# A hybrid mixer layer on one core: whole-row opening loads, dots ahead of the copies, and a planner with one shared transfer pipe

## The chip, the core and the metric

The kernel runs on one core of a Trainium2 chip. A core has a matrix engine (TensorE, PE in the profile), a vector engine (VectorE, DVE), a scalar engine (ScalarE, ACT), a general engine (GpSimd, POOL) and a queue engine (SyncE, SP) that issues most transfers. Operands lie in SBUF, matmul results in PSUM, inputs and outputs in HBM. The metric is the device time of the one program in microseconds, as the median of several runs. A separate profiled execution supplies the trace.

## The reference

The kernel computes one decoder layer and a final norm for a sequence of 1024 tokens and 1024 channels, in float32. Cut to what matters:

```
mod = silu(c) @ mod_w + mod_b                     # 1024 x 3072
shift, scale, gate = split(mod, 3)
h = rmsnorm(x, norm_g) * (1 + scale) + shift
u = h @ w_in                                      # 1024 x 5120
cv, cg, cs, lx, ls = split(u, 5)
v = causal_depthwise_conv(cv * sigmoid(cg), 31 taps)
v = silu(layernorm(v))
y_conv = (v @ pw2_w + pw2_b) * silu(cs)
xs = causal_depthwise_conv(lx, 4 taps)
r, i = sigmoid(block_diagonal(xs))                # two gates, 8 heads
hs = linear_scan(a = exp(-8 r softplus(-lam)), sqrt(1 - a*a) * i * xs)
y_lru = hs * silu(ls)
x = x + (1 + gate) * (concat(y_conv, y_lru) @ w_out)
return rmsnorm(x, final_g)
```

## The kernel before

Channels lie on the 128 partitions and tokens along the free dimension, so the 1024 x 1024 activations are eight tiles of 128 x 1024. Every float32 product is made from rounded parts: an operand is split into a high part (a cast on ACT, `hi`) and a remainder (a subtraction on DVE or POOL, `lo`), and a product takes three matmuls, high by high, high by remainder and remainder by high. A weight tile therefore costs a load, a cast (`whi`) and a subtraction (`wlo`), and six matmuls of 512 columns for each of eight channel tiles.

The work has these stages.

1. **Opening.** For each channel tile k three loads come in: 128 rows of the scale matrix (`s`k, tile `modw`), the input (`x`k) and the weights of the first four output tiles (`w`k or, two at a time, `W`k, tile `fraw`). `LOADS` gives their order. c, after silu, is spread over all partitions by 16 small matmuls into PSUM (`spread_c`, tile `c_row`), and ACT copies it to SBUF (`sc`). A dot of `modw` with the spread gives the scale of the channel tile (`dot`; `first_dot` for tile 0 reads PSUM directly, in two halves). From it follows `gs`, then `uh` and `ul`, the high part and remainder of x times `gs`. With them PE makes the products `first` (line 747). Small matmuls of ones (`idle_mm`, `IDLE` of them) keep PE busy before that. The first tile of x comes in two halves of 512 tokens and w0, w1 in separate loads.
2. **Row norm.** Squares of x are summed, PE sums them over channels and spreads the reciprocal root over partitions (`token_stats`, `rbc`). The shift matrix (`h`0 to `h`7) is dotted in the same way, and three further weight tiles (`NEXT`) are run on the scaled input before the shifted input `hh`, `hl` exists.
3. **Slots.** The list `slots` runs over the remaining tiles of w_in, the gates of the eight recurrence heads (`gates`) and the eight lru tiles of w_out. PE works through them one after another (line 472). The evacuations, the depthwise convolutions (`conv_tile`), the gates and the scans run beside it on ACT and DVE. In three of eight convolutions (`POOLED`) ACT makes the tap products and POOL-issued transfers add them up in SBUF; the last three operations fold them together (`FOLD`). Eight dots for the output gate run in the slots from `GM` on (`gate_mod`, engine `GDOT`). Weight remainders of the slots before number `EARLY` are made on POOL.
4. **Normalisation and pw2, then w_out.** The eight convolution tiles are added to `csum` in the order `SUMS`, then come mean, variance and silu, and the two remaining projections as pair products with fewer multiplications (`pair_products`, line 594; `papw` and `pbpw` are its PSUM tiles for pw2).
5. **End.** The last norm is made for the token ranges in `END`. For the last range `rstd` sums the squares with matmuls and spreads the reciprocal root (`spread`, line 685, tile `finbc`). ACT copies `finbc` to SBUF (`bc`) for the two tiles of channels that POOL finishes, and DVE reads `finbc` for the other six.

The order on every engine is not written by hand. Each operation is registered with an engine, an estimated cost, a priority and its reads and writes, and `Plan.order` simulates the five engines and puts the ready operation of lowest priority number next. `until` holds the time at which an engine is free, `done` the time at which a result is there, `releases` the buffers that come free. There are 47 large SBUF buffers, three PSUM tiles of two banks (`mm`) and two of one (`acc`). In the simulation of before an SP load occupies SP for its bytes, and the accumulating transfers of POOL have a pipe of their own (`adder`). Names such as `RES`, `HRES` and `SPARE` are buffers that stay in reserve when an operation asks for one.

Of the kernel before, what the change touches and what calls it, by code (L numbers as in the profile page):

```python
# [33 lines left out]
NEXT = (("in", LS), ("in", CS), ("in", CS + 1))  # L34
EW = FW + len(NEXT) * P
# [20 lines left out]
SUMS = (0, 1, 3, 2, 6, 4, 7, 5)  # L56
QRES = 4
AHEAD = 4
IDLE, IDLE0 = 15, 4
WARM = (5, 2)  # L60
LANDING, MARGIN = 5.0, 2.0
SP0 = 3.6
SPP = 30
PAD = 16
GLO = "DVE"
GDOT = "DVE"
FOLD = "DVE"
EARLY = 10
ISSUE, FLIGHT, RATE = 1.0, 10.0, 3.5
GM = 22  # L70
TAPP = -15
# [5 lines left out]
LOADS = "s0 x0 w0 s1 x1 w1 W2 s2 x2 s3 x3 W4 s4 x4 s5 x5 W6 s6 x6 s7 x7 h0 h1 h2 h3 h4 h5 h6 h7".split()  # L77
# [20 lines left out]
class Plan:  # L98
# [5 lines left out]
    TICK, BUSY = 3.4133, 3060  # L104

    def __init__(self, pools):
        self.pools = pools
        self.ops, self.writer, self.readers, self.adder = [], {}, {}, 0.0
# [46 lines left out]
    def order(self):  # L155
# [3 lines left out]
        until = {"PE": 1.0, "ACT": 2.0, "DVE": 2.9, "POOL": 1.1, "SP": SP0}  # L159
# [4 lines left out]
        releases, out, table, t, ticks = [], [], None, 0.0, {}  # L164
# [34 lines left out]
        while left:  # L199
# [3 lines left out]
            for e in engines:  # L203
# [69 lines left out]
def hymba_layer(ctx: ExitStack, tc: tile.TileContext, xT, vecs, mod_w, w_first, w_in,  # L273
# [137 lines left out]
    extra = {0: [2, 3], 1: [4], 2: [5], 3: [6], 4: [7]}  # L411
    late_cs = {5, 6, 7}
    for i in range(KT):
        slots.append(("in", LX + i))
        if i > 0:
            slots.append(("in", LS + i))
        if ("in", CS + i) not in NEXT and i not in late_cs:
            slots.append(("in", CS + i))
        if i == KT - 1:
            slots.append(("in", CS + 5))  # L420
        slots.append(("gate", i))
        for j in extra.get(i, []):
            slots += [("in", CG + j), ("in", CV + j)]
    slots += [("in", CS + 6), ("in", CS + 7)]
# [239 lines left out]
    def rstd(prio, sqs, a, e, ps, o, after=(), warm=()):  # L664
# [6 lines left out]

        idle = mm_tile("idle") if warm else None
# [10 lines left out]
        def spread():  # L683
# [11 lines left out]
        return wk, S.op("PE", 0.22 * nb, spread, prio, [rs], wk, columns=4 * P * nb)  # L695
# [64 lines left out]
    for i, ld in enumerate(LOADS):  # L760
# [6 lines left out]
        elif ld[0] in "wW":  # L767
# [6 lines left out]
            for j in range(k, k + nk):  # L774
                due[f"w{j}"] = p
                jj = j % 2
                ACT(p, fw_part(hi, j), fw_part(rw, j), "copy", FW, r=[(rw, jj)], w=[(hi, jj)])
                SUB(p, "DVE", fw_part(lo, j), fw_part(rw, j), fw_part(hi, j), FW,
                    r=[(rw, jj), (hi, jj)], w=[(lo, jj)])
        else:  # L780
            for a, e in START if k == 0 else ((0, T),):
                DMA(p + 1.5 * (k == 0 < a), part(xt[k], a, e), lambda k=k, a=a, e=e: xT[k * P:(k + 1) * P, a:e],
# [15 lines left out]
    def first_dot(p):  # L798
# [12 lines left out]
    for z in (0, 1):  # L811
        ACT(-101, half(sc, z), half(ps_c[z], 0), "copy", H, r=[ps_c[z]], w=[(sc, z)])
    begun, uhs, uls, scaled, split_u, last_u = {}, [], [], [], [], {}
    for k in range(KT):
        p = due[f"s{k}"]
        a_ = col(macc, KT + k)
        if k == 0:
            first_dot(p)
        else:
            dot(SCALE[k], p, KT + k, split_u[:1] if k == 1 else [])  # L820
        S.op("DVE", 0.2, lambda k=k, a_=a_: dve.scalar_tensor_tensor(
# [59 lines left out]
    for k, sq in enumerate(sqs):  # L881
        S.op("PE", 0.23 * KT, lambda sq=sq, k=k: stats(sq, k), RSP, [sq], wk,
# [4 lines left out]
    for a, e in START:  # L887
        spread = S.op("PE", 0.22 * ((e - a) // P), lambda a=a, e=e: spread_mm(a, e), RSP,
                      [("st", 0)], wk, columns=4 * (e - a))
        ACT(RSP, part(rbc, a, e), part(psb, 0, e - a), "copy", e - a, r=wk,  # L890
            w=halves(rbc, a, e))
# [571 lines left out]
```

## Time and profile before

| | |
|---|---|
| median of 3 runs | 741.27 us (740.9 to 742.06) |
| the profiled execution | 741.66 us |
| its span, first to last instruction | 739.8 us |
| granted TensorE clock over the span | 0.997 |
| busy in the span | PE 728.5, DVE 637.9, ACT 441.4, POOL 115.1 us |
| HBM read, written | 64.16 MB, 12.58 MB |

A row of the timeline holds the start and the duration in microseconds, the engine, the line of the kernel, the operation, what it writes and reads, and in brackets the idle time before it and what ended that. A row of the groups holds a count, the busy time and the mean in nanoseconds, then the idle time before the group. Matmuls overlap in the pipeline: one of 512 columns is shown as 0.39 us while the next starts 0.23 us later. "PEld" is the loading of weights into PE, "SPq" the queue of SP. Tile names in the profile stand without their numbers.

### The profile page before, as it was taken

The page shows a single profiled execution, that of the slowest core. Times are in us where ns is not written, and L with a number is a line of the kernel's source. Part 1 is how long each engine was busy: PE and PEld are TensorE (multiplying, and loading weights), DVE is VectorE, ACT ScalarE, POOL GpSimd, SP SyncE. Part 2 cuts the span into 40 slices and gives each one's busy share as a digit, 9 for nine tenths or more (in the row PEclk, how much of TensorE's full clock was granted, in tenths as well). Part 3 has the DMA queues.
Part 4 walks back from the last instruction along what each step waited for, and adds up shares of the span by engine and source line. Part 5 has one row for each costly group of instructions (what it writes and reads, how often), then busy time and mean ns, then how long its engine had stood idle before and what let it go on. Part 6 is the DMA issues. An engine that isn't in the chain of part 4 may idle for free.

```text
span 739.8 us, 8931 instructions
## 1 busy us (share of the span) xinstructions
PE 728.5 (98%) x3314; PEld 605.0 (82%) x3314; DVE 637.9 (86%) x847; ACT 441.4 (60%) x546; POOL 115.1 (16%) x116
## 2 busy tenths in 40 slices
PE   8999999999999999999999999999999999999996
PEld 7788888887888888888887888878888888877886
DVE  6999999988899788888499997978799867999945
ACT  6570597658867857946939777734754224455422
POOL 0023020220331330432215111010000000000003
PEclk9999999999999999999999999999999999999998
DMA  9953025664798899698872556425233430623206
GB/s 324 400 190 114 0 87 121 148 137 99 137 223 201 197 220 260 163 236 161 177 163 54 127 112 185 153 103 199 86 114 114 172 113 1 227 80 120 86 1 228
DMA packets 37340, 111.59 MB, mean 151 GB/s; under 512 B 4144, under 2 KB 12848, under 8 KB 37296
## 3 DMA queue, kind: packets, MB, share of 16 engines
q1 hardware_dynamic: 23904, 75.97, 29.0%
q0 software_dynamic: 12528, 34.26, 25.8%
q10 hardware_dynamic: 864, 0.79, 0.3%
q8 instruction: 26, 0.43, 0.2%
q14 instruction: 18, 0.15, 0.1%
HBM read 64.16 MB, written 12.58 MB: 104 GB/s over the span
## 4 chain that ended last, share of the span: by engine, by line
PE 88%; DVE 7%; ACT 1%; DMA 1%; issue 1%; SPq 0%; DVEq 0%
PE ps L472 65%; PE papw L594 5%; PE pbpw L594 4%; PE first L747 4%; PE pbout L594 2%; PE paout L594 2%; PE gate L1149 2%; PE out L655 2%; DMA fraw<-in_w_first_dram 1%; DVE fin L336 1%; PE late L747 1%; DVE rawout L344 1%; DVE l34out L344 1%; DVE yu L344 1%; DVE yt L344 0%
## 5 line engine op out<-in xcount | busy, mean ns | idle before, releaser
L472 PE MATMUL ps<-uh,whi 128*128 128x512 f32 x576 | 177.7, 390 | 0.6 <-ACT sls L325 0.6
L472 PE MATMUL ps<-ul,whi 128*128 128x512 f32 x576 | 177.5, 389 | 0.0
L472 PE MATMUL ps<-uh,wlo 128*128 128x512 f32 x576 | 177.5, 389 | 0.0
L472 PEld LDWEIGHTS ps<-uh,whi 128*128 128x128 f32 x576 | 107.9, 188 | 23.6 <-ACT sls L325 1.5
L472 PEld LDWEIGHTS ps<-uh,wlo 128*128 128x128 f32 x576 | 108.1, 188 | 22.5
L472 PEld LDWEIGHTS ps<-ul,whi 128*128 128x128 f32 x576 | 108.1, 188 | 22.4
L317 ACT CAST whi<-raw 128x1024 fp32r<-128x1024 f32 x46 | 48.1, 1051 | 66.1 <-PE ps L472 48.4
L349 POOL DMA_DIRECT2D es<-cq x45 | 40.5, 914 | 164.7 <-ACT cq L325 126.9
L325 ACT ACT_TABLE_LOAD x47 | 60.3, 1283 | 2.1 <-PEq L1455 0.7
L349 POOL DMA_DIRECT2D oo<-co x42 | 39.5, 946 | 122.9 <-ACT co L325 52.2
L344 DVE TENSOR_TENSOR wlo<-raw,whi 128x1024 fp32r<-128x1024 f32 x40 | 48.7, 1219 | 10.8 <-ACT whi L317 10.6
L336 DVE SCALAR_TENSOR_TENSOR cacc<-v,V,cacc 128x511 f32<-128x511 f32 (+14 forms) x75 | 55.8, 744 | 0.4
L336 DVE SCALAR_TENSOR_TENSOR caccs<-c,wsum,caccs 128x511 f32<-128x511 f32 (+6 forms) x70 | 52.1, 745 | 3.4 <-ACT caccs L325 2.4
L336 DVE SCALAR_TENSOR_TENSOR caccs<-v,V,caccs 128x511 f32<-128x511 f32 (+6 forms) x70 | 52.2, 746 | 0.9
L344 POOL TENSOR_TENSOR o<-fin,bc 128x256 f32<-128x256 f32 (+1 forms) x8 | 7.3, 938 | 244.6 <-ACT bc L317 244.6
L472 PE MATMUL ps<-yh,whi 128*128 128x512 f32 x128 | 40.1, 394 | 0.0
L472 PE MATMUL ps<-yl,whi 128*128 128x512 f32 x128 | 39.5, 390 | 0.0
L472 PE MATMUL ps<-yh,wlo 128*128 128x512 f32 x128 | 39.4, 389 | 0.0
L325 ACT ACTIVATE cq<-v,V 128x511 f32<-128x511 f32 (+14 forms) x45 | 31.6, 706 | 0.2 <-DMA es<-cq 0.2
L336 DVE SCALAR_TENSOR_TENSOR xs<-ps,V,xs 128x1023 f32<-128x1023 f32 (+2 forms) x24 | 30.6, 1276 | 0.1
L325 ACT ACTIVATE cq<-c,wsum 128x512 f32<-128x512 f32 x42 | 29.7, 711 | 0.0
L325 ACT ACTIVATE co<-v,V 128x511 f32<-128x511 f32 (+13 forms) x42 | 29.0, 706 | 0.0
(328 smaller groups left out, 1439.0 us busy)
## 6 DMA issues: line engine op xcount, KB each, us to landing
raw<-in_w_in_dram SPq DMA_DIRECT2D x36, 512.0 KB, 4.8
modw<-in_mod_w_dram SPq DMA_DIRECT2D x24, 512.0 KB, 7.7
raw<-in_w_out_dram SPq DMA_DIRECT2D x10, 512.0 KB, 3.9
scsd<-scs SPq DMA_DIRECT2D x8, 512.0 KB, 3.4
acc<-in_xT_dram SPq DMA_DIRECT2D x8, 512.0 KB, 4.9
accd<-acc SPq DMA_DIRECT2D x8, 512.0 KB, 2.8
rawpw<-in_pw_dram SPq DMA_DIRECT2D x8, 512.0 KB, 3.6
scsr<-scsd SPq DMA_DIRECT2D x8, 512.0 KB, 5.6
```

The lines of the kernel that those rows point to most:

```text
L317: act.copy(out(), in_())
L325: act.activation(out=out(), in_=in_(), func=func, **kw)
L336: dve.scalar_tensor_tensor(out=out(), in0=in0(), scalar=scalar, in1=in1(), op0=op0, op1=op1, accum_out=accum)
L344: lambda: e.tensor_tensor(out=out(), in0=a(), in1=b(), op=op), prio, r, w,
L349: return S.op("POOL", ISSUE, lambda: pool.dma_start(out(), a(), accum_op=ALU.add), prio, r, w, lag=RATE * n / T, after=after)
L472: pe.matmul(ps()[:, a - off:b - off], k3(lhs)()[:, k, :], rhs[k]()[:, a:b], start=(k == 0 and lhs is wh and rhs is xh and (a - off) % H == 0),
L594: pe.matmul(half(*ps)(), half(*lhs)()[:, j * P:j * P + P], half(*rhs)(), start=start and j == 0 and z == 0, stop=j == KT // 2 - 1 and z == ...
L655: pe.matmul(ps()[:, a - off:e - off], k3(lhs)()[:, k, :], rhs()[:, i * H + a % H:i * H + a % H + e - a], start=k == KORD[0] and lhs is wh ...
L747: pe.matmul(ps()[:, a - off:b - off], fw_part(lhs, k, i * P, i * P + P)(), rhs()[:, a:b], start=k == 0 and lhs is wh and rhs is xh, stop=k ...
L1149: pe.matmul(ps()[:, c0:c1], lhs()[:, j, :], rhs()[:, c0:c1], start=st == 0, stop=st == 2)
```

## The change

The change has three kinds of parts.

- *Opening.* x0 is loaded in one transfer of whole rows instead of two halves, and w0 and w1 come in one load (`W0`). The ACT copies of the spread are registered after the dots that read it in PSUM. Each later scale dot follows the `gs` step of the tile before it.
- *Planner.* All transfers, those of SP and the accumulating ones of POOL, share one simulated pipe (`self.pipe`); SP runs ahead of it by at most `BACKLOG`. PE is taken to be at half clock before 4.7 us. Several constants change with it: engine start times, reserves, `ORDER` in place of the loop that wrote the slot list (it differs in that the sigmoid tile 15 comes before slot 28 and tile 7 after gate 4), `SUMS`, `EARLY`, `GM`, `IDLE`. The gate dots (`GDOT`) and the folds (`FOLD`) move from DVE to POOL; on POOL a dot is a product there and a summing activation on ACT. Casts of the second and third `NEXT` weights follow the second copy of `rbc`.
- *End.* The last norm's spread is made twice, once into `bc` for DVE and once into another PSUM tile (`b2`) for the ACT copy.

```diff
-    slots (loop over KT with extra and late_cs)
+ORDER = "i24 g0 i10 i2 i11 i3 i25 i33 g1 i12 i4 i26 i34 i18 g2 i13 i5 i27 i35 i19 g3 i14 i6 i15 i28 i36 i20 g4 i7 i29 i37 g5 i30 i38 g6 i31 i39 i21 g7 i22 i23"
-SPARE = 5
+SPARE = 7
-RES = 6
+RES = 2
-HRES = 4
+HRES = 6
-SUMS = (0, 1, 3, 2, 6, 4, 7, 5)
+SUMS = (2, 6, 1, 4, 3, 0, 5, 7)
-IDLE, IDLE0 = 15, 4
+IDLE, IDLE0 = 13, 4
-LANDING, MARGIN = 5.0, 2.0
-SP0 = 3.6
-SPP = 30
+LANDING, MARGIN = 4.0, 2.0
+BACKLOG = 6.0
+SP0 = 1.0
+SPP = 25
-GDOT = "DVE"
-FOLD = "DVE"
-EARLY = 10
-ISSUE, FLIGHT, RATE = 1.0, 10.0, 3.5
-GM = 22
-TAPP = -15
+GDOT = 'POOL'
+FOLD = 'POOL'
+EARLY = 14
+ISSUE, FLIGHT, RATE = 1.0, 10.0, 3.0
+GM = 14
+TAPP = 15
-LOADS = "s0 x0 w0 s1 x1 w1 W2 s2 x2 s3 x3 W4 ...
+LOADS = "s0 x0 W0 s1 x1 W2 s2 x2 s3 x3 W4 ...
...
-                self.adder = max(self.adder + o.lag, end + FLIGHT)
-                end = self.adder
+                self.pipe = max(self.pipe, end) + o.lag
+                end = max(self.pipe, end + FLIGHT)
+            elif o.eng == "SP":
+                self.pipe = end = max(self.pipe, end - o.cost) + o.cost
+                until["SP"] = max(end - o.cost + 0.4, end - BACKLOG)
...
-                    if ticks.get(int(t / self.TICK) - 1, 0) < self.BUSY:
+                    if t < self.COLD or ticks.get(int(t / self.TICK) - 1, 0) < self.BUSY:
...
+        if idle:
+            S.op("PE", 0.22 * nb, lambda: spread(idle), prio, [rs], [idle], after=[op],
+                 columns=4 * P * nb)
...
-            for a, e in START if k == 0 else ((0, T),):
-                DMA(p + 1.5 * (k == 0 < a), part(xt[k], a, e), ...
+            for a, e in ((0, T),):
+                DMA(p, part(xt[k], a, e), ...
...
-            STT(p, part(m, a, e), part(m, a, e), 1.0, half(ps_c[z], 0), ALU.mult, ALU.mult, H,
+            o = STT(p, part(m, a, e), part(m, a, e), 1.0, half(ps_c[z], 0), ALU.mult, ALU.mult, H,
                 accum=to, r=[(m, z), ps_c[z]], w=[(m, z), key])
+            ACT(-101, half(sc, z), half(ps_c[z], 0), "copy", H, r=[ps_c[z]], w=[(sc, z)],
+                after=[o])
...
-            dot(SCALE[k], p, KT + k, split_u[:1] if k == 1 else [])
+            dot(SCALE[k], p, KT + k, [gs_op])
...
-        weights(s, where="all", late=[root])
+        weights(s, where="all", late=[root if s == NEXT[0] else spread_out])
...
+        b2 = mm_tile("idle") if e == T else bc
-        rstd(n, [ss, qz], a, e, bc, 0, warm=WARM if e == T else ())
+        rstd(n, [ss, qz], a, e, bc, 0, warm=WARM if e == T else (), idle=b2 if e == T else None)
-        ACT(n + 0.2, part(bs, 0, w_), part(bc, 0, w_), "copy", w_, r=[bc], w=[bs])
+        ACT(n + 0.2, part(bs, 0, w_), part(b2, 0, w_), "copy", w_, r=[b2], w=[bs])
```

More of the change, by code (lines that the diff above doesn't have):

```diff
@@ L158, in order @@
         engines = ("PE", "ACT", "DVE", "POOL", "SP")
-        until = {"PE": 1.0, "ACT": 2.0, "DVE": 2.9, "POOL": 1.1, "SP": SP0}
+        until = {"PE": 1.0, "ACT": 2.5, "DVE": 2.6, "POOL": 1.1, "SP": SP0}
         pending = {e: [] for e in engines}
@@ L163, in order @@
                 pending[o.eng].append(o)
-        releases, out, table, t, ticks = [], [], None, 0.0, {}
+        releases, out, table, t, ticks = [], [], "silu", 0.0, {0: self.BUSY}
         held = {"DVE": 0.0, "POOL": 0.0}
@@ L410, in hymba_layer @@
     slots = list(FIRST + NEXT)
[L411 to L424, printed above, removed]
+    for x in ORDER.split():
+        slots.append(("gate" if x[0] == "g" else "in", int(x[1:])))
     slots += [("lru", m) for m in range(KT)]
@@ L661, in tail_mm, with rstd @@
                     columns=3 * (e - a))
-    def rstd(prio, sqs, a, e, ps, o, after=(), warm=()):
+    def rstd(prio, sqs, a, e, ps, o, after=(), warm=(), idle=None):
         nb = (e - a) // P
@@ L681, in stats, with spread @@
                           skip_group_check=True)
-        def spread():
+        def spread(ps=ps):
             for b in range(nb):
@@ L889, in hymba_layer @@
                       [("st", 0)], wk, columns=4 * (e - a))
-        ACT(RSP, part(rbc, a, e), part(psb, 0, e - a), "copy", e - a, r=wk,
-            w=halves(rbc, a, e))
+        spread_out = ACT(RSP, part(rbc, a, e), part(psb, 0, e - a), "copy", e - a, r=wk,
+                         w=halves(rbc, a, e))
     fsum, bias = big_buf("fsum", parts=2), ctile("bias", len(FIRST + NEXT))
@@ L1209, in hymba_layer @@
             if (a, e) in cuts[i]:
-                TT(p, "DVE", part(t, a, e), part(ps, a, e), part(rbc, a, e), ALU.mult, n,
-                   r=pk + halves(rbc, a, e), w=tk)
+                TT(p - 4 * (len(cuts[i]) == 1), "DVE", part(t, a, e), part(ps, a, e),
+                   part(rbc, a, e), ALU.mult, n, r=pk + halves(rbc, a, e), w=tk)
             else:
```

23 lines of the change are left out of this document (11 added, 12 removed).

## The prediction

> **What bounds the kernel now.** I read the page's busy table first, then the chain that ended last, then the waits of TensorE (PE), and only then the timeline of the ends of the span.
>
> ```profile
> span 739.8 us, 8931 instructions
> PE 728.5 (98%) x3314; PEld 605.0 (82%) x3314; DVE 637.9 (86%) x847; ACT 441.4 (60%) x546; POOL 115.1 (16%) x116
> PE 88%; DVE 7%; ACT 1%; DMA 1%; issue 1%; SPq 0%; DVEq 0%
> ```
>
> PE is busy for 728.5 of 739.8 us and carries 88% of the chain. Only 11.3 us of the span can be won by ordering alone, since the change takes no product away. The waits say where they lie (engine, line, released by: us in total, times, longest).
>
> ```profile
> PE first L747 <- ACT fhi L317: 0.9, 1, 0.9
> PE pbout L594 <- DVE fin L336: 0.8, 1, 0.8
> PE paout L594 <- ACT eout L317: 0.7, 1, 0.7
> PE ps L472 <- ACT sls L325: 0.6, 2, 0.3
> PEld first L747 <- DVE ul L336: 1.0, 2, 0.7
> ```
>
> Behind the opening the matmul rows lose only 2.1 us (0.8 + 0.7 + 0.6). The last row is the weight loader's: two losses in the opening. The rest of the 11.3 us is the time before the first product and the tail after the last. So the opening decides; here it is, with the transfer rate in four windows (start:end, length, five engines' busy time, clock, DMA share, GB/s).
>
> ```profile
> 1.17 0.42 SPq L363 DMA_DIRECT2D modw<-in_mod_w_dram  x1
> 4.44 1.28 ACT L325 ACT_TABLE_LOAD   x1
> 5.85 1.05 ACT L317 COPY sc<-c_row 128x512 f32<-128x512 f32 x2
> 6.45 0.69 DVE L336 SCALAR_TENSOR_TENSOR modw<-modw,c_row 128x512 f32<-128x512 f32 x1 [3.60 <-ACT sc L317]
> 7.06 0.68 DVE L336 SCALAR_TENSOR_TENSOR modw<-modw,c_row 128x512 f32<-128x512 f32 x1
> 8.12 0.49 DVE L358 TENSOR_SCALAR uh<-x,gs 128x512 fp32r<-128x512 f32 x1
> 8.44 0.62 ACT L317 CAST fhi<-fraw 128x512 fp32r<-128x512 f32 x1 [1.54 <-DMA fraw<-in_w_first_dram]
> 9.11 1.19 PE L747 MATMUL first<-uh,fhi 128*128 128x512 f32 x4 [0.87 <-ACT fhi L317]
> 12.17 0.17 DVE L358 TENSOR_SCALAR sp_s<-sp_u 128x8 f32<-128x8 f32 x1
> 12.35 0.62 ACT L317 CAST fhi<-fraw 128x512 fp32r<-128x512 f32 x1 [1.51 <-DMA fraw<-in_w_first_dram]
> 19.84 0.50 PE L747 MATMUL first<-ul,fhi 128*128 128x512 f32 x1 [0.26 <-DVE ul L336]
> ...
> L363 SPq DMA_DIRECT2D modw<-in_mod_w_dram x1: 421/421/421, 1.2 to 1.2; - x1
> ...
> DMA to landing us min/median/max: 3.3/3.3/3.3
> ...
> 4.50:7.00 2.50, 2.50 (x24) 2.50 (x23) 0.55 (x1) 2.39 (x4) 0.00 (x0) 1.00 0.94 209
> 7.00:8.50 1.50, 1.24 (x12) 1.05 (x10) 1.43 (x7) 0.06 (x1) 0.00 (x0) 1.00 0.98 384
> 8.50:10.00 1.50, 0.89 (x4) 0.75 (x5) 1.01 (x3) 1.39 (x3) 0.00 (x0) 1.00 1.02 414
> 20.00:30.00 10.00, 10.00 (x45) 8.24 (x46) 10.00 (x18) 6.66 (x11) 0.00 (x0) 1.00 1.03 408
> ```
>
> Two chains meet at the first product (9.11). Weights: w0 lands at 8.42 (8.44 less the start delay), its cast takes 0.62. Inputs: the first dot starts at 6.45, released by the ACT copy out of the same PSUM tile, though its matrix landed at 1.2 + 3.3 = 4.5; ACT itself was late because of the table load at 4.44. While w0 and the half of x travel, the queue's share is 0.94 but it moves 209 GB/s; with whole 4 KB rows behind it 408 to 414. In the last window DVE is as busy as PE (10.00 of 10.00), so PE can keep a head start only if DVE gets one too.
>
> **The change, part by part.**
>
> *Loads of whole rows.* Before: matrix, half of x0, w0 alone, other half of x0. After: matrix, x0 (0.52 MB), w0 and w1 together (0.52 MB). At 414 GB/s 0.52 MB takes 1.27 us, so the pair lands at 4.5 + 2 x 1.27 = 7.0 instead of 8.4: 1.4 us earlier. At the 209 GB/s of the window in which it travels it lands at 4.5 + 5.0 = 9.5, 1.1 later. I take 7.0, nearest to the rows that carry 4 KB rows, and keep +1.1 for the range. SP issues two transfers fewer; nothing waits for its queue here.
>
> The Trainium skill, DMA: Bandwidth & Descriptors, Specifications, puts the smallest transfer at line rate at 512 B. By that rule 2 KB rows aren't slow, the 209 GB/s belongs to the first microseconds, and the pair lands at 9.5. No row here parts the two.
>
> *Dots before the copies.* The ACT copies of the spread now come after the dots. The first dot can start when the matrix is there (4.5) and the spread's first half is written, the second when the last spread matmul is done:
>
> ```profile
> 2.96 2.83 PE L717 MATMUL c_row<-ident,cs 128*128 128x128 f32 x16
> ```
>
> that is at 5.8, against 7.06. From the second dot's start to the end of uh took 8.12 + 0.49 - 7.06 = 1.55, so inputs are ready at 7.35; weights (7.0 + 0.62 + 0.07 = 7.7) remain the later chain. First product 9.11 - 1.4 = 7.7, and DVE, which waited for the same cast, is 1.4 early as well: **-1.4**. The matrix dot for the next tile now waits for the copies behind the dots (5.8 + 0.7 + 1.05 = 7.6 at most); its own matrix lands at 8.3, so that wait is covered. Two idle products fewer keep PE warm a little less (a gap of some 0.2 us, before it was 0.87); zero.
>
> *w1 with w0.* The cast at 12.35 waited for w1, and DVE filled in with the small softplus steps from 12.17 on; this chain ends in the two losses on ul. With w1 there by 7.0 they should go: between 0 and 1.0 (the loader's row), 0.3 by the PE row alone at 19.84; I take **-0.5**.
>
> *A second spread at the end.* The last rows now:
>
> ```profile
> 732.37 0.71 PE L685 MATMUL finbc<-ident,rs64.6_0_5676 128*128 128x128 f32 x4 [0.15 <-DVE rs64.6_0_5676 L694]
> 733.12 0.37 ACT L317 COPY bc<-finbc 128x256 f32<-128x256 f32 x1 [1.15 <-PE finbc L685]
> 733.52 2.44 DVE L336 SCALAR_TENSOR_TENSOR o<-fin,V,finbc 128x256 f32<-128x256 f32 x6 [1.21 <-ACT bc L317]
> 733.57 1.41 POOL L344 TENSOR_TENSOR o<-fin,bc 128x256 f32<-128x256 f32 x2 [1.57 <-ACT bc L317]
> 735.00:738.50 3.50, 0.00 (x0) 0.00 (x0) 0.96 (x3) 0.00 (x0) 0.00 (x0) 0.51 0.87 292
> ```
>
> DVE's six outputs wait for the ACT copy of the same tile. With a copy of the spread of its own for ACT, DVE starts at 733.1, 0.4 earlier. The four extra matmuls (at most 0.71) delay ACT and POOL to 734.3 + 1.41 = 735.7, level with DVE's new end of 735.56. The stores behind them keep the queues at 0.87, so not all comes through: 0 to 0.4, I take **-0.3**.
>
> *Work moved to POOL* (gate dots, the last folds of three conv tiles, four more weight remainders):
>
> ```profile
> L336 DVE SCALAR_TENSOR_TENSOR modw<-modw,sc 128x1024 f32<-128x1024 f32 x23 | 27.9, 1218 | 0.0
> L344 POOL TENSOR_TENSOR wlo<-raw,whi 128x1024 fp32r<-128x1024 f32 x6 | 14.6, 2461 | 50.1 <-DVE fsum L336 47.3 <-ACT ghi L317 1.9 <-ACT whi L317 1.0
> L344 POOL TENSOR_TENSOR csum<-csum,c 128x1024 f32<-128x1024 f32 x5 | 13.5, 2701 | 29.1 <-DVE c L344 28.9
> 51.38 2.35 DVE L358 TENSOR_SCALAR sp_q<-sp_q 128x8 f32<-128x8 f32 x1
> ```
>
> Twelve whole operations go from 1.22 on DVE to 2.46 on POOL, nine half-width folds from about 0.6 to about 1.3 (half of 1.22, half of 2.70). DVE is spared 12 x 1.22 + 9 x 0.6 = 20 us; it gains PE nothing where PE doesn't wait for it. POOL gets 12 x 2.46 + 9 x 1.3 = 41 us more on 115: room enough, but its accumulating transfers queue behind each operation by up to 2.46. ACT gets eight sums of a row, 8 x 1.05 (the copy of as many elements at 5.85) = 8 us on 441. On the path: 0; if the cover goes, see the third rival. The row at 51.38 is a step of 0.17 us that took 2.35 while POOL worked, so a part of the sparing is paid back.
>
> The Trainium skill, SBUF — State Buffer, Who interferes with whom, says that the port pair which DVE and GpSimd share is an exclusive lock held for a whole instruction. The row at 51.38 agrees; by the rule alone DVE would lose up to those 41 us for the 20 it is spared, 21 us of its 102 idle ones.
>
> *The planner's numbers and the slot order* (one sigmoid tile three slots earlier, buffer reserves, one pipe for all transfers) move instructions but add none. Their price isn't in this trace. The three waits behind the opening bound the gain at -2.1; a new collision costs about as much as one of them, 0.3 to 0.8, so a handful makes +3. I take 0, for want of a row that favours either side.
>
> Sum: -1.4 - 0.5 - 0.3 = **-2.2 us**. The profiled execution took 741.66 us (739.8 of span and 1.9 around it), 0.4 above the median of 741.27. Taking the difference: 741.66 - 2.2 = 739.5 profiled, 741.27 - 2.2 = **739.1** as median.
>
> **The rivals.**
>
> *The replanning helps too.* The three waits behind the opening are places where an evacuation came late; a planner that sees transfers truly may remove most. For it: they are order, not work. Against: at the two longest DVE has no free time, as the stretch of one of them shows (DVE is the third busy time). 739.1 - 2.1 = 737.0.
>
> ```profile
> 640.00:660.00 20.00, 19.33 (x86) 15.69 (x85) 20.00 (x30) 9.31 (x13) 0.00 (x0) 1.00 0.22 79
> ```
>
> *The slow rate belongs to the first microseconds.* The pair lands at 9.5, the first product is at 10.2 (+1.1), the losses on ul still go, the tail stays: +1.1 - 0.5 - 0.3 = +0.3, 741.6. For it: the other half of x0 is 2 KB rows too, and the window with it reaches 384. Against: that window also holds 4 KB rows.
>
> *The convolution's sum comes late* (the other side).
>
> ```profile
> 489.04 1.22 DVE L344 TENSOR_TENSOR csum<-csum,c 128x1024 f32<-128x1024 f32 x1
> 568.25 5.44 PE papw L594 x24
> 570.45 1.22 DVE L344 TENSOR_TENSOR vlc<-vt,vhc 128x1024 fp32r<-128x1024 f32 x1
> ```
>
> All eight tiles must be summed before mean and normalisation, and these before pw2's products at 568.25. The row at 568.25 holds two products, 2.72 each. The last operand of the third (573.7) is made at 571.7: 2.0 us of slack. The new order sums tile 6 second and puts five POOL additions (2.70 each) behind it, tile 5 with its folds on POOL (0.7 more for each of three) among them. If tile 6 or 5 is done when the last was before, up to 5 x 2.7 = 13.5 us stand ahead of the last addition; each us beyond 2.0 is one us of PE. It decides against the change from 2.0 + 2.2 + 1.5 = 5.7 us on; a slip of 8 us gives 739.1 + 6.0 = 745.1, of 5.7 us 742.8. Against: PE has other tiles to run until 568, and the additions behind tile 6 may lie before the last tile is done.
>
> **How the numbers follow.** A run can tell some 0.2% (1.5 us) from no change, so faster is below 739.8 and slower above 742.8. Forecast 0.45 (own range 738.2 to 740.2, nine tenths of it faster), replanning helps 0.22 (faster), slow first microseconds 0.12 (same), late sum 0.21 (three quarters slower, else same). Faster 0.40 + 0.22 = 0.62; same 0.05 + 0.12 + 0.05 = 0.22; slower 0.16. The range leaves out 0.04 below the second case's outer end and 0.15 of the late sum's long tail: 736.4 to 742.2.
>
> **What would show it.** Right: the first product near 7.7, its cast released by fraw near 7.0; the rate between 4.5 and 7 about 400; no copy named ahead of the first dot; fewer than 0.5 us of loader waits for ul; the first of the last six outputs within 0.1 us of the spread's end. Wrong: PE waits behind 100 us of more than 4 us in all, a wait of papw or pbpw near 568, or DVE busier than 638 us beside POOL. If the opening is early and the time is not, the gain was given back in the middle.

## The result, and the profile after

The change made the kernel slower: 745.55 us (median of 6 runs, 744.68 to 748.03) against 741.12 us (median of 6) on the same chip, a ratio of 1.0062 with a 95% interval of 1.0047 to 1.0077. That is +4.4 us where -2.2 was forecast; the predicted 739.1 and its range (to 742.2) both miss. One execution each of two experiments below (moved work on DVE, loads alone) took 3270 and 2632 us, with a granted clock of 1.00 on record, for a reason that nothing here shows; both are left out, and since the first is the only profiled execution of its kernel, that kernel's trace isn't used.

The profiled execution of the kernel after is its slowest, 748.03 us (span 746.2). Read its rows for the mechanism; the prices come from the timed runs of the experiments.

From the page of the kernel after: the span, the busy times, and the shares of the chain that ended last.

```profile
span 746.2 us, 8914 instructions
PE 731.5 (98%) x3314; PEld 607.0 (81%) x3314; DVE 640.8 (86%) x818; ACT 446.6 (60%) x560; POOL 165.4 (22%) x137
PE 80%; DVE 14%; issue 2%; ACT 2%; DMA 1%; SPq 0%; DVEq 0%; ACTq 0%
```

PE now carries 80% of the chain, before 88%; DVE's share has doubled from 7 to 14%. DVE is busier than before (637.9), although work was taken from it, and POOL has gained 50 us. The waits of PE name the place (engine, line, released by: us in total, times, longest).

```profile
PE late L742 <- DVE first_u L349: 2.8, 1, 2.8
PE first L742 <- ACT fhi L322: 2.0, 1, 2.0
PE pbout L587 <- DVE fin L341: 0.8, 1, 0.8
PE paout L587 <- ACT eout L322: 0.7, 1, 0.7
PE ps L465 <- ACT scs L330: 0.7, 1, 0.7
PE gate L1145 <- DVE xsl L349: 0.5, 1, 0.5
```

The first row is new: it doesn't stand among PE's waits in the kernel before. There only the weight loader shows a short wait at this place, for ACT. These are its row and three of the timeline of before, then the row of after:

```profile
PEld late L747 <- ACT rbc L317: 0.5, 1, 0.5
53.15 0.59 ACT L317 COPY rbc<-token_stats 128x512 f32<-128x512 f32 x1
53.79 0.50 PE L747 MATMUL late<-uh,fhi 128*128 128x512 f32 x1
55.57 2.49 DVE L344 TENSOR_TENSOR first_u<-first,rbc 128x512 f32<-128x512 f32 x4
```

```profile
57.82 0.50 PE L742 MATMUL late<-uh,fhi 128*128 128x512 f32 x1 [2.75 <-DVE first_u L349]
```

`late` is the accumulator of the second half of the fourth output tile, whose 24 products close the opening. In the list above, the second row was 0.9 before. The others are small: 2.7 us in all, where the rows behind the opening made 2.1.

The opening, and its windows (start:end, length, busy time of PE, its loader, DVE, ACT and POOL with counts, clock, DMA share, GB/s):

```profile
4.93 0.69 DVE L341 SCALAR_TENSOR_TENSOR modw<-modw,c_row 128x512 f32<-128x512 f32 x1 [2.04 <-DMA modw<-in_mod_w_dram]
6.72 0.49 DVE L363 TENSOR_SCALAR uh<-x,gs 128x512 fp32r<-128x512 f32 x1
8.87 0.62 ACT L322 CAST fhi<-fraw 128x512 fp32r<-128x512 f32 x1 [1.82 <-DMA fraw<-in_w_first_dram]
9.54 0.73 PE L742 MATMUL first<-uh,fhi 128*128 128x512 f32 x2 [1.96 <-ACT fhi L322]
```

```profile
4.50:7.00 2.50, 2.50 (x25) 2.50 (x24) 1.96 (x7) 2.49 (x4) 0.00 (x0) 1.00 0.91 282
7.00:8.50 1.50, 0.58 (x6) 0.39 (x4) 0.96 (x2) 0.05 (x1) 0.00 (x0) 1.00 0.96 325
8.50:10.00 1.50, 0.46 (x2) 0.42 (x3) 0.48 (x1) 1.13 (x2) 0.00 (x0) 1.00 1.03 410
10.00:15.00 5.00, 5.00 (x17) 3.92 (x16) 4.50 (x11) 3.67 (x7) 0.00 (x0) 0.66 1.03 420
50.00:65.00 15.00, 12.25 (x55) 10.08 (x54) 12.28 (x17) 5.74 (x9) 8.03 (x4) 0.89 0.26 93
```

The first dot waits for its matrix and for no copy, and the inputs are ready at 6.72 + 0.49 = 7.21. The weights are not: the pair lands at 8.85. PE idles 1.96 us and works at a clock of 0.66 between 10 and 15. In the last window PE loses 15.00 - 12.25 = 2.75 us again, and the clock falls again (0.89). These are the rows of that place, from the timeline:

```profile
49.96 2.91 POOL L349 TENSOR_TENSOR wlo<-raw,whi 128x1024 fp32r<-128x1024 f32 x1 [48.64 <-DVE modw L341]
50.66 2.21 DVE L898 TENSOR_TENSOR shift<-macc,V 128x1 f32<-128x1 f32 x1
54.48 2.41 POOL L349 TENSOR_TENSOR wlo<-raw,whi 128x1024 fp32r<-128x1024 f32 x1 [1.62 <-ACT whi L322]
54.61 2.30 DVE L898 TENSOR_TENSOR shift<-macc,V 128x1 f32<-128x1 f32 x1
57.09 1.87 DVE L349 TENSOR_TENSOR first_u<-first,rbc 128x512 f32<-128x512 f32 x3
```

PE starts `late` at 57.82, when the first of the three evacuations at 57.09 (some 0.7 each) is done. DVE comes to it late: two additions of one element per partition, 0.15 us at other places, took 2.21 and 2.30, each ending when a POOL remainder ends. And the tail:

```profile
738.97 0.71 PE L676 MATMUL finbc<-ident,rs64.6_0_5681 128*128 128x128 f32 x4
739.72 2.44 DVE L341 SCALAR_TENSOR_TENSOR o<-fin,V,finbc 128x256 f32<-128x256 f32 x6 [0.81 <-PE finbc L676]
```

Set side by side, the two profiled executions say where the 6.4 us between the spans come from:

| point (us) | before | after | after less before |
|---|---|---|---|
| first product | 9.11 | 9.54 | +0.4 |
| `late` starts | 53.79 | 57.82 | +4.0 |
| products of the first slot start | 59.37 | 65.03 | +5.7 |
| mean of the convolution | 490.58 | 497.23 | +6.7 |
| last spread | 732.37 | 738.97 | +6.6 |
| end of the span | 739.8 | 746.2 | +6.4 |

Nearly all of it is in by 65 us. At `late` PE loses 2.9 from one product's start to the next, before 0.2; behind that it runs ten products at about 0.43 us from start to start, not 0.23, some 1.8 more. The early clock loss of this execution is about 1.6, and the middle, 65 to 497 us, adds 1.0.

### The profile page after: what moved, and what is told of

Same layout as the page of the kernel before. It is cut to its first block, busy times and chain, and to the rows that moved or that the text cites. A ratio compares the mean times of both kernels' runs of the same rounds, so it can differ in the third digit from the quotient of the medians.

```text
span 746.2 us, 8914 instructions
## 1 busy us (share of the span) xinstructions
PE 731.5 (98%) x3314; PEld 607.0 (81%) x3314; DVE 640.8 (86%) x818; ACT 446.6 (60%) x560; POOL 165.4 (22%) x137
## 4 chain that ended last, share of the span: by engine, by line
PE 80%; DVE 14%; issue 2%; ACT 2%; DMA 1%; SPq 0%; DVEq 0%; ACTq 0%
PE ps L465 58%; PE papw L587 4%; PE first L742 4%; PE pbpw L587 3%; PE gate L1145 2%; PE pbout L587 2%; PE paout L587 2%; PE out L648 2%; DVE wlo L349 1%; PE late L742 1%; DVE caccs L341 1%; DMA fraw<-in_w_first_dram 1%; DVE xs L341 1%; DVE fin L341 1%; DVE modw L341 1%
## 5 line engine op out<-in xcount | busy, mean ns | idle before, releaser
L349 DVE TENSOR_TENSOR wlo<-raw,whi 128x1024 fp32r<-128x1024 f32 x36 | 54.4, 1510 | 6.0 <-ACT whi L322 6.0
L354 POOL DMA_DIRECT2D oo<-co x42 | 41.8, 1026 | 47.2 <-ACT co L330 25.1
L349 POOL TENSOR_TENSOR wlo<-raw,whi 128x1024 fp32r<-128x1024 f32 x10 | 25.0, 2504 | 119.5 <-ACT whi L322 65.5
## 6 DMA issues: line engine op xcount, KB each, us to landing
x<-in_xT_dram SPq DMA_DIRECT2D x8, 512.0 KB, 10.8
```

The costliest lines, as they stand in the source:

```text
L349: lambda: e.tensor_tensor(out=out(), in0=a(), in1=b(), op=op), prio, r, w,
L354: return S.op("POOL", ISSUE, lambda: pool.dma_start(out(), a(), accum_op=ALU.add), prio, r, w, lag=RATE * n / T, after=after)
```

## The experiments

Theory A: the time is lost at `late`, because of one line of the whole diff that is not among the lines printed above and whose price the prediction never worked out: `TT(p - 4 * (len(cuts[i]) == 1), ...)`. It puts the evacuation of the fourth output tile first on DVE. Two accumulators of this kind exist; one holds that tile's first half and is freed by DVE, the other (`token_stats`) is freed by ACT's copies of the spread. In the order of the instructions before, `late` waits for ACT; in the one after, for DVE. Rivals: the clock lost in the gap before the first product (B); the work moved to POOL, which locks DVE out (C).

### The change without the early evacuation

```diff
-                TT(p - 4 * (len(cuts[i]) == 1), "DVE", part(t, a, e), ...
+                TT(p, "DVE", part(t, a, e), ...
```

> The changed kernel without the higher priority of the fourth output tile's evacuation (the 4 that is taken off). Theory, the buffer: the late products took the accumulator that this evacuation frees, and waited 2.75 us for DVE, which then cost half clock from 58.6 to 62.3 (another 1.9). With the evacuation last again they take the buffer that the copy of the row norm frees, start within 0.6 us of the second spread's end, and the time is 2.7 to 4.6 us lower: 740.9 to 742.8. Rival, DVE is late there whatever the buffer, since POOL blocks it for 2.2 us twice: the wait moves to the next product that needs DVE, 745 to 745.5.

Measured: 741.87 us (10 runs), ratio to before 1.0008 (0.9999 to 1.0017): 3.7 us less than the change whole. From its waits and windows:

```profile
PE late L742 <- ACT rbc L322: 0.8, 1, 0.8
50.00:65.00 15.00, 14.19 (x71) 11.88 (x70) 15.00 (x16) 5.27 (x7) 9.42 (x5) 1.00 0.15 49
```

`late` is released by ACT again, 0.8 us late and not 2.8, and the clock stays at 1.00. One line holds five sixths of the loss (3.7 of 4.4). The planner orders the middle otherwise too (the convolution's mean comes at 485.53, not 497.23), and of the 6.3 us between the two profiled executions 1.1 come behind the first slot's start, so a part of the 3.7 may be the new order and not the wait.

### The early evacuation alone

```diff
-                TT(p, "DVE", part(t, a, e), part(ps, a, e), ...
+                TT(p - 4 * (len(cuts[i]) == 1), "DVE", part(t, a, e), part(ps, a, e), ...
```

in the kernel before.

> The kernel before with one edit of the change alone: the fourth output tile of the opening is the first to be evacuated on DVE. Theory A (this edit by itself makes TensorE wait for DVE, because the accumulator of the late products comes from the tile that DVE empties first, at the time when POOL's weight remainders hold DVE up): the late products wait 2 us or more with a half clock behind them, 741.12 + 3.5 = 744.6. Theory B (the edit needs the rest of the change, which has one POOL remainder more at this place): the late products wait less than 0.5 us as before, 741.1 to 741.5. Between the two: the wait is there but under 1.5 us and no half clock follows, 742.2.

Measured: 755.41 us, ratio 1.0190 (1.0176 to 1.0204). The expected wait is there, but the total is 10.8 us past the 744.6 of theory A. The rows, two of the waits of PE, two of DVE's timeline, and the last addition of the convolution:

```profile
PE late L747 <- DVE first_u L344: 2.6, 1, 2.6
PE papw L594 <- DVE vla L344: 2.1, 2, 1.8
```

```profile
48.52 2.48 DVE L336 SCALAR_TENSOR_TENSOR fsum<-raw,shift,fsum 128x128 f32<-128x128 f32 x1
50.91 2.36 DVE L358 TENSOR_SCALAR sp_q<-sp_q 128x8 f32<-128x8 f32 x1
505.99 1.23 DVE L344 TENSOR_TENSOR csum<-csum,c 128x1024 f32<-128x1024 f32 x1
```

At `late` PE loses 2.8, and then eight products at half clock cost 0.2 each: 4.4 us, which is theory A at this place. The two stretched DVE rows stand in the kernel before as well (2.48 at 48.98, 2.35 at 51.38): POOL's lock was there all along and cost PE nothing, since `late` hung on ACT. What the edit adds is that PE hangs on DVE. The other 9.9 us of the 14.3 are elsewhere: the planner, given this one number, ordered the rest otherwise, the convolution's last addition slid from 489.04 to 505.99, and PE starved for the operands of pw2 (9.9 us, summed from start to start of its products between 577 and 592). The next experiment shows that mechanism without the edit.

### The dots before the copies, alone

```diff
-            STT(p, part(m, a, e), ...
+            o = STT(p, part(m, a, e), ...
+            ACT(-101, half(sc, z), half(ps_c[z], 0), "copy", H, ..., after=[o])
...
-    for z in (0, 1):
-        ACT(-101, half(sc, z), half(ps_c[z], 0), "copy", H, r=[ps_c[z]], w=[(sc, z)])
```

in the kernel before.

> The kernel before with the dots ahead of the copies and nothing else. Theory: the inputs are ready 1.4 us earlier, but the weights still land at 8.4 and set the first product, which stays at 9.1; within 0.7 us of 741.3. Rival, DVE is what the opening runs on and its head start is worth something by itself: 740 or less.

Measured: 751.35 us, ratio 1.0131 (1.0114 to 1.0148). Both theories (within 0.7 of 741.3, or 740) miss. In the opening the inputs are ready at 7.24 and the weights, landed at 7.92, set the first product at 8.61. The profiled executions with the opening of before (before, fewer idle products, second spread alone, early evacuation alone) have it at 8.90 to 9.12, in three of the four because the inputs, not the weights, end last; `late` starts at 53.50, in the first three of them at 53.27 to 53.79. So the step gives 0.3 to 0.5 us at the first product and nothing that can be told at `late`. Then the replanned middle (waits of PE, the last addition, and the window of pw2; below it the same window of the kernel before):

```profile
PE papw L594 <- DVE vla L344: 2.1, 2, 1.8
PE papw L594 <- ACT epw L317: 1.4, 1, 1.4
PE papw L594 <- ACT vha L317: 1.2, 2, 0.8
502.07 1.22 DVE L344 TENSOR_TENSOR csum<-csum,c 128x1024 f32<-128x1024 f32 x1
570.00:595.00 25.00, 20.09 (x68) 14.08 (x67) 24.09 (x32) 9.46 (x12) 0.00 (x0) 0.80 0.30 103
```

```profile
570.00:595.00 25.00, 25.00 (x112) 20.72 (x111) 18.12 (x24) 7.68 (x9) 0.00 (x0) 1.00 0.46 164
```

The addition comes 502.07 - 489.04 = 13.0 us later. PE is busy 20.09 of 25 us where it was busy throughout, at a clock of 0.80 and with DVE at 24.09; summed from start to start of its products it loses 9.9 us between 573 and 588. This is the prediction's third rival, in a kernel for which the rival was not written. Its rule (2.0 us of slack, each further us one us of PE) gives 11.0.

### The clock in the opening

```diff
+    def idle_last():
+        for _ in range(1 + MORE):      # MORE = 7
+            idle_mm()
```

emitted in place of the last idle product: once in the change whole, once in the change without the early evacuation.

> The changed kernel with seven more products of ones behind the last one (written into the same step, so that the order on every engine stays as it is). Theory, the clock: PE stood idle for 2.0 us before the first product and then ran at half clock from about 11.0 to 14.4 us. With the gap filled to under 1 us the granted clock of 10 to 15 us is 1.00 and not 0.66, the products after 15 us stand 1.6 us earlier, the first product stays at 9.5, and the time falls from 745.5 to about 743.9. Rival, the gap is harmless and the clock falls for another reason: 0.66 stays, 745.5.

> Both edits. If the two losses are separate, the gains add up: 739.3 to 741.2, with the opening (start of the slots' products) about 0.4 us behind that of the kernel before at worst. If the planner's new order costs on its own in the middle, 742 or more although PE has neither loss before 65 us.

Measured: 745.52 us (4 runs, ratio 1.0053, 1.0033 to 1.0072), and 742.49 us (10 runs, ratio 1.0015, 1.0006 to 1.0025). The window of the first of the two:

```profile
10.00:15.00 5.00, 5.00 (x27) 4.22 (x26) 4.54 (x11) 3.72 (x7) 0.00 (x0) 1.00 1.03 419
```

The clock is 1.00 where it was 0.66, and the median is what it was (745.52 and 745.55). The added products pushed the first real one back to 10.45, 0.9 us later than in the change, so this isn't the cure of a gap at no cost and can't price the early clock by itself. In the kernel without the early evacuation the profiled execution had no gap to fill. Its opening has the same instructions as the change's, but the products of ones ended later and the first product came 0.24 us behind them, at a clock of 1.00:

```profile
6.63 2.62 PE L708 MATMUL token_stats<-ones 128*128 128x128 f32 x18
9.49 1.19 PE L742 MATMUL first<-uh,fhi 128*128 128x512 f32 x4 [0.24 <-ACT fhi L322]
```

So the gap differs between executions of the same opening, and the second pair (742.49 and 741.87) says nothing on it; the 739.3 to 741.2 expected of both edits didn't come, which by that text means that the new order costs something by itself (0.4 to 1.9 us by the interval). What falls is B as the main cause: the first kernel has no early clock loss in its trace, keeps the wait of 2.8 us at `late`, and is as slow; the one without the early evacuation wins 3.7 us with the opening as it was. Whether the half clock at 11 us belongs to every execution of the change, or to the profiled one, these runs don't say.

The other way round, five idle products fewer in the kernel before:

```diff
-        S.op("PE", 0.22, idle_mm, -120, [], [psb], columns=4 * P,
+        S.op("PE", 0.22, idle_mm if i < 10 else (lambda: None), -120, [], [psb], columns=4 * P,
```

> The kernel before with the last five steps of ones left out (the order stays as it is), so that PE stands idle for 2 us before the first product as in the profiled execution of the changed kernel. If such a gap can bring a stretch at half clock, some executions are 1.6 us slower than 741.3 and others are not, and a granted clock below 1 stands between 10 and 15 us where it fell. If the gap is harmless, all executions stay within 0.7 us of 741.3.

Measured: 741.19 us (10 runs), ratio 1.0001 (0.9991 to 1.0010). The gap before the first product was 1.01 us, not the 2 us aimed at, the clock behind it 1.00, the time the same. So a gap as long as that of the change was not tried.

### What is slow in the loads

First the order of the transfers in the change whole, the weight pair ahead of everything:

```diff
-LOADS = "s0 x0 W0 s1 x1 W2 ...
+LOADS = "W0 s0 x0 s1 x1 W2 ...
```

> The changed kernel with the weights' pair loaded first, then the matrix, then x0. Theory, the weights' first transfer is itself slow: the first transfer lands 1.5 us later than the 4.8 us at which the matrix landed, at 6.3 or later, and the other two follow 1.3 us apart. Rival, the time between 5.5 and 8.5 us is slow for any transfer: the weights land at 4.8, the matrix at 6.1, and x0 is the slow one and lands near 8.8. The time itself stays within 1.5 us of 745.5 by either.

Measured in a single execution: 751.6 us, where a time within 1.5 of 745.5 was expected. The first product came only at 11.69 and the order behind it is another, so the total says nothing on the loads. The landings do: the pair at 6.26, where the matrix, when it was first, landed at 4.82, so 1.4 later for the same bytes; then the matrix at 8.21 (1.95 behind the pair) and the input tile at 9.46 (1.25). In the change itself the gaps were 1.26 for the input tile and 2.76 for the pair; the next pair took 1.28. Most of the loss went with the weights to the front, but the matrix behind them lost 0.7 too, in the stretch of 6 to 8.5 us in which the pair is slow in the change.

Then a touch: one transfer of 4 KB in all from the weight block on ACT's queue, ahead of everything there, in the change without the early evacuation. The order of all other work stays.

```diff
+    seen = const.tile([P, 8], F32, tag="seen", name="seen"); act.dma_start(seen, w_first[:, 0, 0:8])
```

> The kernel after with the ordinary evacuation order (741.87), plus one added transfer on ACT's queue, ahead of all else on that queue: 8 columns of the first weight block, 4 KB in all, into a buffer that nobody reads. The order of all other instructions stays. The weight pair landed 2.4 to 2.8 us after the input tile where 0.52 MB of other data take 1.25 to 1.28. Theory A (the first transfer that touches the weight tensor is slow, whoever sends it): the pair lands about 1.3 us behind the input tile, near 7.6, the first product is near 8.4 (0.62 for the cast and 0.1 behind it), 741.87 - 1.1 = 740.8. Theory B (a big transfer is slow there whatever came before it): landing near 8.8 as before, first product near 9.5, 741.9. Theory C (the added transfer pushes the loads back): landing later than 8.8, above 742.0.

Measured: 741.63 us (11 runs), ratio 1.0007 (0.9999 to 1.0016).

```profile
8.18 0.62 ACT L322 CAST fhi<-fraw 128x512 fp32r<-128x512 f32 x1 [0.81 <-DMA fraw<-in_w_first_dram]
8.85 1.21 PE L744 MATMUL first<-uh,fhi 128*128 128x512 f32 x4 [0.84 <-ACT fhi L322]
```

The pair landed 1.77 us behind the input tile, without the touch 2.44; the first product came at 8.85, without it at 9.49. That is half of the excess over 1.26 gone. But these are single executions, and those without a touch differ among themselves: the five kernels that load the pair third gave 2.76, 2.63, 2.53, 2.44, and 1.90 for the one that follows. In the time the 0.6 us are hardly seen (741.87 to 741.63).

Last, the whole loads alone, in the kernel before:

```diff
-LOADS = "s0 x0 w0 s1 x1 w1 W2 ...
+LOADS = "s0 x0 W0 s1 x1 W2 ...
...
-            for a, e in START if k == 0 else ((0, T),):
+            for a, e in ((0, T),):
```

> The kernel before with the loads of the change alone: x0 in one transfer of whole rows, the first two weight pieces in one. Theory, the first transfer of the weights costs 1.5 us beyond its bytes wherever it stands: the pair lands near 8.8, its first product starts 0.4 us later than 9.11, the wait for the second piece is gone, and the time is within 0.7 us of 741.3. Rival, the prediction's: the pair lands near 7.0, the first product starts at 7.7, 739.4.

Measured: 742.97 us, ratio 1.0023 (1.0014 to 1.0033). Here the pair landed at 7.77, and still the first product came at 10.52:

```profile
8.29 0.72 ACT L325 ACTIVATE uh<-x,gs 128x512 fp32r<-128x512 f32 x1 [1.21 <-DVE gs L821]
8.92 1.04 ACT L325 ACTIVATE sq<-x 128x1024 f32<-128x1024 f32 x1
9.86 1.12 ACT L317 CAST fhi<-fraw 128x512 fp32r<-128x512 f32 x2
```

ACT had two operations on the input tile ahead of the cast in its queue, and both stood behind the dots that wait for the copies. Neither theory's landing (8.8 or 7.0) came. Whole loads without the other step cost 1.8 us (741.21 before on the same chip): a case in which an order on one engine, not the transfer, sets the start.

### The work moved to POOL

```diff
-GDOT = 'POOL'
-FOLD = 'POOL'
-EARLY = 14
+GDOT = 'DVE'
+FOLD = 'DVE'
+EARLY = 10
```

in the change without the early evacuation.

> The changed kernel with the evacuation last again (741.9) and with the gate dots, the folds and the four weight remainders back on DVE. Theory, the port: the move to POOL spares DVE about as much as POOL's hold of the port takes from it, and PE waits for neither; DVE's mean for a weight remainder falls from 1.5 to 1.22 us, the time stays within 1 us of 741.9. Rival, the move costs by blocking DVE where PE waits: 740.5 or less. Rival on the other side, it was worth something: 743.5 or more.

Measured: 743.56 us, ratio 1.0029 (1.0019 to 1.0039), against 1.0008 (0.9999 to 1.0017) with the work on POOL. Theory C falls as far as the moved work goes: the move doesn't cost, it gains 1.7 us, as far as one comparison of two plans can tell. POOL's hold on DVE stays a part of theory A: by the rows of after, the two stretched steps took 2.1 us each more than their 0.15, ahead of the evacuation for which PE waits 2.75. It doesn't need the moved work, since the early evacuation alone brings the wait in the kernel before; the change whole with this work back on DVE was not run. What it spares DVE is much less than the 20 us counted. The groups of one operation, a weight remainder of the same shape on DVE (busy us, mean ns), before, after, and in the change without the early evacuation:

```profile
L344 DVE TENSOR_TENSOR wlo<-raw,whi 128x1024 fp32r<-128x1024 f32 x40 | 48.7, 1219 | 10.8 <-ACT whi L317 10.6
```

```profile
L349 DVE TENSOR_TENSOR wlo<-raw,whi 128x1024 fp32r<-128x1024 f32 x36 | 54.4, 1510 | 6.0 <-ACT whi L322 6.0
```

```profile
L349 DVE TENSOR_TENSOR wlo<-raw,whi 128x1024 fp32r<-128x1024 f32 x36 | 48.4, 1344 | 14.3 <-ACT whi L322 14.3
```

Four instructions fewer, and as much or more time in all, since each takes longer. DVE's whole busy time went from 637.9 to 640.8 in the change and to 632.3 without the early evacuation.

### The second spread at the end, alone

```diff
+        if idle:
+            S.op("PE", 0.22 * nb, lambda: spread(idle), prio, [rs], [idle], after=[op], ...
...
-        ACT(n + 0.2, part(bs, 0, w_), part(bc, 0, w_), "copy", w_, r=[bc], w=[bs])
+        ACT(n + 0.2, part(bs, 0, w_), part(b2, 0, w_), "copy", w_, r=[b2], w=[bs])
```

in the kernel before.

> The kernel before with the second spread at the end alone; the order up to the last spread stays. My step: the first of the last six outputs on DVE starts within 0.1 us of the end of the spread that it reads (before: 0.45 after it), the time from the start of the last spread to the end of the span falls from 7.43 us by 0.3 (bounds 0 to 0.4), so 741.12 - 0.3 = 740.8. Rival: the copy on ACT and the two POOL outputs, which now wait for the second set of matmuls, end last and the tail grows by up to 0.3: 741.4.

Measured: 740.98 us (11 runs), ratio 0.9998 (0.9989 to 1.0007).

```profile
731.82 0.71 PE L684 MATMUL finbc<-ident,rs64.6_0_5676 128*128 128x128 f32 x4 [0.15 <-DVE rs64.6_0_5676 L693]
732.57 2.44 DVE L336 SCALAR_TENSOR_TENSOR o<-fin,V,finbc 128x256 f32<-128x256 f32 x6 [0.80 <-PE finbc L684]
```

The outputs start 0.04 us after the spread's end (0.44 before), and from the spread's start to the end of the span it is 738.9 - 731.82 = 7.1 us (739.8 - 732.37 = 7.4 before). The step is right to its size, and below what the timed runs can tell from nothing.

### The parts that won, in the kernel before

The second spread and the touch together; the order of all else is that of before.

> The kernel before with the two parts that won something by themselves and leave the order of all other work alone: the second spread at the end (740.98 alone) and the small early transfer from the weight tensor (landing of the weight pair 0.6 us earlier, time 0.24 less on the kernel after with the ordinary evacuation). Theory A (the gains add, and in the kernel before the weights end last at the first product): w0 lands 0.5 to 0.7 us earlier behind the half of the input tile than the 2.29 us of before, the first product follows, 740.98 - 0.3 = 740.7. Theory B (the inputs end last in the kernel before, their dots waiting for the copies, as soon as the weights come earlier): the weights land earlier and the first product does not, 741.0.

Measured: 740.80 us (11 runs), before on the same chip 741.26, ratio 0.9995 (0.9986 to 1.0004). It has the lowest median of all kernels here, by an amount that isn't told from no difference.

```profile
7.33 0.62 ACT L317 CAST fhi<-fraw 128x512 fp32r<-128x512 f32 x1 [0.23 <-DMA fraw<-in_w_first_dram]
8.19 0.49 DVE L358 TENSOR_SCALAR uh<-x,gs 128x512 fp32r<-128x512 f32 x1
8.83 1.16 PE L750 MATMUL first<-uh,fhi 128*128 128x512 f32 x4
```

The first weight block lands 0.86 us behind the half input tile; in the five kernels with the same loads and no touch it was 1.68 to 2.29. The half input tile itself took 1.76 here (1.05 to 1.66 there), so a part of the loss only moved; the block lands at 7.31, without the touch at 7.81 to 8.42. Now the inputs are last (8.19 + 0.49 = 8.68): theory B of this expectation, as far as the start goes.

## Why the prediction was wrong, by its steps

- **The step that failed: the planner's numbers and the slot order, put at 0.** The prediction listed what this step moves and priced a collision by the waits it saw, 0.3 to 0.8. The line that brings the fourth tile's evacuation forward stood in the whole diff and in none of the steps. It made PE depend on DVE for an accumulator that ACT used to free. Measured: a 2.9 us step where there was 0.2, then about 1.8 of half clock; 3.7 us in the timed runs, more than the +3 that a handful of collisions was to cost. The rows of before had the warning: the 2.35 us of the small step at 51.38 showed DVE held up at this place, and `late` starts at 53.79, ahead of the first evacuation. The prediction used that row only to discount the sparing on DVE.
- **Loads of whole rows, -1.4.** Wrong by 1.8: the pair landed at 8.85, not 7.0, though the input tile took the 1.26 us of whole rows that the step assumed. The slow rate was put on 2 KB rows, and the pair has 4 KB rows and is slow. The Trainium skill's rule cited there (DMA: Bandwidth & Descriptors, Specifications: 512 B as the smallest transfer at line rate) agrees with that. The second rival, which put the rate on the first microseconds, was right in direction, and the kept bound of +1.1 was not reached (the first product came 0.4 late). What the rate hangs on isn't settled: the loss follows the weights to the front of the queue and shrinks with a touch, which speaks for the first transfer from that tensor; the 0.7 that the matrix loses behind them, and the 1.90 of one kernel without a touch, don't fit that alone.
- **Dots before the copies.** Right in itself: inputs ready at 7.21 (forecast 7.35), no copy ahead. Worth nothing while the weights end last; alone in the kernel before, 0.3 to 0.5 us at the first product and none seen at `late`. The two idle products fewer were put at 0 for a gap of 0.2 us. In the profiled execution the gap was 1.96, with some 1.6 us of half clock behind it; with the same opening it was 0.24 in another kernel's. What they cost by themselves no run shows.
- **w1 with w0, -0.5.** Right: the two losses on `ul`, together 0.5 from start to start of PE's products, are gone from the trace.
- **A second spread, -0.3.** Right: 0.2 in the change, 0.3 alone.
- **Work moved to POOL, 0.** Better than forecast: about 1.7 us gained. The statement of the Trainium skill cited there (SBUF — State Buffer, Who interferes with whom: the shared port as an exclusive lock) agrees with the rows: steps of 0.15 us took 2.2 to 2.4 beside POOL, and the sparing of 20 us became 5.6, or minus 2.9.
- **The late sum of the convolution.** Not in the change: its last addition is at 495.68, 6.6 later than before like everything around it, and no wait of papw shows. With one part of the change alone it happened twice, at 9.9 us each time (by the rule 11.0 with the dots alone, and 11.3 with the early evacuation alone, less the 3.65 us by which its slots start later).
- **Of the list of signs**, three of a right forecast held (no copy ahead of the first dot, no loader waits for `ul`, the last outputs next to the spread) and two did not: the first product stood at 9.54, not near 7.7, and the rate between 4.5 and 7 us was 282, not about 400. Of the marks of a wrong one only DVE's time showed (640.8, above 638). PE's waits behind 100 us stay under 4; the one that counted stood at 55 us, where the list didn't look.

Of the 4.4 us, 3.7 are shown by undoing one line. The remaining 0.7 (0.9999 to 1.0017 as a ratio) is within what the runs can tell from nothing. Forecast and measurement lie 6.6 us apart (-2.2 and +4.4); the early evacuation (3.7) and the mis-sized loads (1.8) make 5.5 of them, and these runs don't share out the rest.

## What to carry to other kernels

When an evacuation is moved forward, ask which product is handed the buffer that it frees, and which engine now releases that product: a product moved from a free engine's release to a busy one's can lose more than the whole change was to win. Read a line that changes one priority as a change of dependencies, and price it like one. In a kernel whose order a planner makes, a part tried alone brings an order of its own (9.9 us lost at another place here, twice, from edits of a few lines), so keep the order fixed where a part's own price is wanted, or read that price at its place in the trace rather than from the total.

## What the runs showed of the hardware

- The first pair of weights, loaded third behind the matrix and the input tile, took 1.90 to 2.76 us for 0.52 MB, where the transfer of that size ahead of it took 1.26 to 1.30, and those from the second behind it on 1.26 to 1.29. With an early touch of 4 KB it took 1.77. No run shows why.
- A wait of 2.6 to 2.8 us of PE at `late` was followed by half clock in all three kernels that had one (after, with more idle products, early evacuation alone), for eight to ten products; a wait of 1.9 us at the same place (weights first) was not. Ahead of the first product, gaps of 1.96 (after) and 3.1 us (weights first) were followed by half clock, gaps of 1.01 (fewer idle products) and 1.63 us (loads alone) were not. Each is one execution. The Trainium skill, TensorE: Matmul & The Clock Gate, Part 1, has the clock fall after an idle window of about 3.4 us; here 2.75 us within a longer stretch of work were enough.
- A DVE instruction of one element per partition ended only when the POOL instruction beside it ended (2.21 and 2.30 us against 0.15 at other places).
